# A two-layer trunk in split fp32: the second MLP matrices' first pairs taken as wide seven-product pairs

## The chip, the cores and the metric

One Trainium2 chip, one core. The metric is the device time of one execution in microseconds (us); the kernel is launched once and computes the whole reference. TensorE is called PE (PEld is its weight load), VectorE DVE, ScalarE ACT, GpSimd POOL, and SyncE SP; nearly all loads are issued from SP.

## The reference

256 rows of 2048 channels go through two layers, all in float32. Cut to its steps:

```python
# layer 1
u = rms_norm(h, a_norm_g);  q, k, v, fz = split(u @ a_w_in)          # 2048 -> 3*2048+16
h = h + forgetting_attention(norm(q), norm(k), v, log_sigmoid(fz + b_f)) @ a_w_out
h = h + square(relu(rms_norm(h, g0) @ w1[0])) @ w2[0]                # 2048 -> 8192 -> 2048
# shared keys and values
k_sh, v_sh = split(rms_norm(h, kv_norm_g) @ kv_w)
# layer 2
q = norm(rms_norm(h, b_norm_g) @ b_w_q)
h = h + chunked_relbias_attention(q, norm(k_sh), v_sh, b_rel) @ b_w_out
h = h + square(relu(rms_norm(h, g1) @ w1[1])) @ w2[1]
```

The change concerns the second products (w2) of the two MLPs.

## The kernel before

**Products.** Weights are the moving operand of PE, 128 x 512 at a time; activations, transposed, are the stationary one, as 16 tiles x[0] to x[15] of 128 channels by 256 rows. Both are split into a part hi that PE takes exactly and the rest lo, and each product is made of three passes: hi by hi, hi weights by lo activations, lo weights by hi activations (lines L462, L464, L466, in `passes`). The weights are split as they arrive: ACT writes hi (L218) and DVE writes lo (L219). A **unit** is a block of weights of 128 x 1024 (512 KB) and takes 12 matmuls: two channel tiles, two row halves, three passes. There are three buffers for hi and three for lo of whole units, and one each for half blocks (`hih`, `loh`). `top_up` splits up to three units ahead; raw units are loaded through four buffers.

**Pairs.** An MLP goes through four chunks c of 2048 hidden channels. Each chunk has four pairs: two of w1 (q = 0, 1), then two of w2 (q = 0, 1). A pair makes two neighbouring results of 512 columns, a and b, over 16 input tiles. On the first input tiles it uses seven products of block sums in place of eight (Winograd's form of Strassen's method) on four blocks of weights "11", "12", "21", "22". The blocks' sums are formed on chip: T3 = 22 + 12, T2 = T3 + 11, T1 = 12 + 11, T4 = 21 + T2. The seven products come as **forms** f0 to f6 in the order 11, T3, T2, T1, 21, T4, 22. The activations' sums for them are called S (w1) and Sh (w2).

- A **narrow** pair does this on four tiles (x[0] to x[3]): f0 to f6 of 6 matmuls each, then the ordinary units a2 to a7 and b2 to b7. Blocks have 512 KB, and all four sums are added by DVE (`make`, L811).
- A **wide** pair does it on six tiles (x[0] to x[5]): each form f_i is followed by a half form h_i of 3 matmuls on a half block; the ordinary units are a3 to a7 and b3 to b7. Blocks have 768 KB. DVE makes T3 and T2, of 128 x 1536; T1 and T4 are made by transfers on POOL's queue that add a block from memory onto the one on chip (`put`, L817).

`WIDE1` and `WIDE2` say which pairs of w1 and w2 are wide: before, all of w1 but the first, and in w2 those with q = 1. The w2 pairs with q = 0, one in each chunk, are narrow.

**Order.** `Pair.plan` writes out the order of units; b5, b6, b7 of a pair come between the first forms of the next pair. The start of a wide pair after a w1 pair reads: ... a7 b3 b4 of the old pair, f0 h0, b5 of the old, f1 h1, b6, f2 h2, b7, f3 h3, then a3 of the new pair. `when` gives for "12", "22", "21", "11", T3, T1 how many ordinary units ahead of the pair's f0 each is loaded or made (`prepare`). `keep_order` makes DVE, ACT, PE and SP keep the written order.

**Hidden activations.** A result of w1 gives a quarter n (0 to 3) of the chunk's hidden tiles: n = 0 and 1 from a and b of the first w1 pair, 2 and 3 from the second. Quarter n holds tiles x[4n] to x[4n+3]. When its sums are done, `turn_hidden` transposes it on DVE (L330), sends it through memory and back, and runs the steps of `take`: relu (ACT, L830), square into hi (ACT, L835), square in place (ACT, L837), lo (DVE, L841), and for n = 0 and 1 four differences (DVE, L285 to L288), their hi part (ACT, L292) and lo part (DVE, L295) in Sh. `uses` says after which ordinary unit each step is written; the numbers count from the transposes.

Of the kernel before, what the change touches and what calls it, by code (L numbers as in the profile page):

```python
# [31 lines left out]
REL = 384  # L32
WIDE = UN + 512
WIDE1 = (1, 2, 3, 4, 5, 6, 7)
WIDE2 = (1, 3, 5, 7)


def keep_order(tc, engines):
# [8 lines left out]


@with_exitstack
def trunk(ctx: ExitStack, tc: tile.TileContext, xT, xr, gs, hg, bf, wgate, w_in, w_oa, w1a, w1fa, w1sa, w2a, w2fa, w2sa,  # L50
          w_kv, w_qb, w_ob, w1b, w1fb, w1sb, w2b, w2fb, w2sb, rel, out):
    nc = tc.nc
    V, S, G, TE, SY = nc.vector, nc.scalar, nc.gpsimd, nc.tensor, nc.sync

# [47 lines left out]
    def queue(src, m):  # L102
        u = [src[i] for i in range(m)]
        n = KT // UA
        u[: 2 * n] = [u[i + q * n] for i in range(n) for q in range(2)]
        units.extend(u)
# [13 lines left out]
    class Pair:  # L120
# [9 lines left out]

        def plan(self, rest):
            made = [self.items(f"f{i} h{i}" if self.wide else f"f{i}") for i in range(7)]
            own = {"early": "a2 F a3 F b2 F b3 a4 b4 a5 a6 a7", "": "a2 F a3 F a4 F a5 a6 a7 b2 b3 b4",
                   "late": "a2 F a3 F b2 F b3 a4 a5 b4 a6 a7", "wide": "a3 F b3 F a4 F b4 a5 a6 a7", "ahead": "a3 F a4 F a5 F a6 a7 b3 b4"}[self.order].split()
            plan = made[0] + rest[:1] + made[1] + rest[1:2] + made[2] + rest[2:] + made[3]
            n = 4
            for i in own:
                if i == "F":
                    plan += made[n]
                    n += 1  # L140
                else:
                    plan += self.items(i)
            return plan, self.items("b5 b6 b7")

    def plan_mlp(w1, w1f, w1s, w2, w2f, w2s, tail):
        pairs = []

        def add(w, wf, ws, i, wides, order, when):
            j = wides.index(i) if i in wides else i - sum(1 for k in wides if k < i)
            names = ("11", "12", "21", "22")  # L150
            if i in wides:
                src = [[None] * 3 + [ws[10 * j + 5 * q + u] for u in range(5)] for q in range(2)]
                big = {k: wf[4 * j + m] for m, k in enumerate(names)}
            else:
                src = [[w[16 * j + 8 * q + u] for u in range(8)] for q in range(2)]
                big = {k: src[int(k[1]) - 1][int(k[0]) - 1] for k in names}
            pairs.append(Pair(big, src, order, len(pairs) % 2 == 0, when, i in wides))

        close = (7, 5, 6, 4, 3, 2)
        for c in range(NCH):  # L160
            for q in range(2):
                i = 2 * c + q
                order = "ahead" if i in WIDE1 else "" if i else "early"
                when = (25, 20, 9, 15, 10, 8) if not i else (9, 7, 8, 6, 3, 2) if i == 1 else close if i - 1 in WIDE1 or not q else (9, 7, 8, 6, 5, 1)
                add(w1, w1f, w1s, i, WIDE1, order, when)
            for q in range(2):
                i = 2 * c + q
                add(w2, w2f, w2s, i, WIDE2, "wide" if q else "late", close if q or i + 1 in WIDE1 else (9, 7, 8, 6, 5, 2))
        plan, rest = [], [(tail, 0, u) for u in range(KT // UA - 3, KT // UA)]
        for p in pairs:  # L170
            mine, rest = p.plan(rest)
            plan += mine
        plan += rest
        units.extend(Form(p, i, q == 3) if q > 1 else p.src[q][i] for p, q, i in plan)
        return plan

# [2 lines left out]
    n_out = w_oa.shape[0] - 3  # L179
    queue(w_oa, n_out)  # L180
    tail_a = Tail(w_oa, n_out - 5)
    plan_a = plan_mlp(w1a, w1fa, w1sa, w2a, w2fa, w2sa, tail_a)
    queue(w_qb, w_qb.shape[0])
    for i in range(w_kv.shape[0]):
        units.append(w_kv[i])
    queue(w_ob, n_out)
    tail_b = Tail(w_ob, n_out - 5)
    plan_b = plan_mlp(w1b, w1fb, w1sb, w2b, w2fb, w2sb, tail_b)
    ready = deque()

    raws = deque()
# [106 lines left out]
    def room(tag, name, dtype=F32):  # L298
        return qkv.tile([P, WIDE], dtype, name=name, tag=tag, bufs=1 if tag == "bias" else 2)
# [18 lines left out]
    def steps(make):  # L318
        box = []

        def step():
            if not box:
                box.append(make())
            next(box[0])
        return step

    def blocks32(src, z, b):
        n = src.shape[1] // P
        nb = z.shape[1] // (n * P)
        V.transpose(z.rearrange("p (j n b c) -> p b n j c", j=4, n=n, b=nb)[:, b],  # L330
                    src.rearrange("p (n j c) -> p n j c", n=n, j=4))

    def carry(z, dst, wait=1):
        w = z.shape[1]
        n = w // 4
        box = []

        def rows():
            box.append(dram.tile([P, w], F32, name="turn", tag=f"turn{w}", bufs=4))
            SY.dma_start(box[0], z)  # L340

        def columns():
            s = box[0].rearrange("(i a) f -> a i f", i=4)
            d = dst.rearrange("p (i f) -> p i f", i=4)
            for j in range(4):
                SY.dma_start(d[32 * j : 32 * j + 32], s[:, :, j * n : (j + 1) * n])

        return [[rows]] + [[]] * wait + [[columns], [], []]

    def turned(name=None):  # L350
        z = qkv.tile([P, GH * T], F32, name="z")
        return (z, qkv.tile([P, GH * T], F32, name=name, tag=name, bufs=2)) if name else z
# [52 lines left out]
    class RowStats:  # L405
# [4 lines left out]
        def add(self, b, n):  # L410
            t = wk.tile([P, 512], F32, name="sqr", tag="wk")
            S.activation(t, h[b][:, n * 512 : (n + 1) * 512], AF.Square, accum_out=self.ss[:, b * NG + n : b * NG + n + 1])
# [250 lines left out]
    def add_fill(items):  # L663
        for i, it in enumerate(items):
            if i < len(fill):
                fill[i] = fill[i] + it
            else:
                fill.append(it)
# [35 lines left out]
    early = room("bias", "early")  # L704
# [75 lines left out]
    for g in range(NG):  # L780
        zq, lq = turned("z")
        qb = {}
        late = 6 if g == 0 else 0
# [35 lines left out]
    def prepare(p, d):  # L819
        for name, at in zip(("12", "22", "21", "11", "T3", "T1"), p.units):  # L820
            if d == at:
                (bring if name[0] != "T" else put if p.adds and name == "T1" else make)(p, name)

    def mlp(plan, x, Sx, st, last):
        base = turns[0]
        hids = [[] for _ in range(NCH)]
        Sh = [[] for _ in range(NCH)]

        def take(t, c, n):
            S.activation(t, t, AF.Relu)  # L830
            y = acts.tile([P, 2, GH, T], F32R, name="act")
            hi, lo = (y[:, i].rearrange("p k (b i c) -> p (k b) i c", b=NB, i=4) for i in range(2))
            t3 = t.rearrange("p (i kb c) -> p kb i c", i=4, c=32)
            yield
            S.activation(hi, t3, AF.Square)  # L835
            yield
            S.activation(t, t, AF.Square)  # L837
            yield

            def low():  # L840
                V.tensor_tensor(lo, t3, hi.bitcast(F32), op=ALU.subtract)  # L841

            hids[c].extend(y[:, :, j, :] for j in range(GH))
            low()
            yield
            if n == 0:
                r = prob.tile([P, 9 * 3 * P], F32R, name="Sh", tag="p", bufs=1)
                Sh[c].extend(r[:, i : i + n] for i, n in ((0, UN), (UN, UN), (2 * UN, 512), (2 * UN + 512, 512)))
                yield from sums([[t3[:, 2 * j + b :: 4] for j in range(2)] for b in range(NB)], Sh[c])
            elif n == 1:  # L850
                yield from sums([[t3[:, 2 * j + b : 2 * j + b + 1] for j in range(2)] for b in range(NB)], Sh[c][2:], 1)

        def turn_hidden(c, n):
            zt = []

            def f(b, ps):
                if b == 0:
                    zt.extend(turned("q"))
                blocks32(ps, zt[0], b)
                if b == NB - 1:  # L860
                    step = steps(lambda: take(zt[1], c, n))
                    uses = ((4, 5, 7, 8, 9, 10, 11), (4, 5, 6, 7, 8, 10, 15), (4, 5, 7, 8), (4, 5, 6, 6))[n]
                    if not c and n < 2:
                        uses = (5, 6, 7, 8, 8, 10, 15) if n else (4, 5, 6, 7, 8, 9, 10)
                    add_fill(carry(*zt, 0)[:2] + [[step] * uses.count(i) for i in range(3, uses[-1] + 1)])
            return f

# [192 lines left out]
```

## Time and profile before

| what | value |
|---|---|
| median of 3 runs (lowest, highest) | 2097.52 us (2096.82, 2102.56) |
| the profiled execution's own time | 2096.35 us |
| its span on the core | 2094.6 us |
| PE busy | 2087.4 us, 9266 records |
| DVE, ACT busy | 1606.3 us, 1233.0 us |
| mean transfer rate | 251 GB/s |

The profile tells one execution. A timeline row holds the start in us from the span's start, the duration of the group, engine, line, operation, out<-in, how many, and in brackets the idle time before it and what ended it. Consecutive rows of PE overlap, because matmuls are pipelined: the step from one start to the next is what a matmul costs, and the 389 ns of a group row is its latency. On DVE the step from one start to the next is also a little shorter than the duration.

### The profile page before, as it was taken

To read this page: it belongs to the slowest core of one execution; us is meant where nothing else is said; L and a number is where in the kernel's file an instruction comes from. 1 tells how busy PE (TensorE), PEld (TensorE's weight loads), DVE (VectorE), ACT (ScalarE), POOL (GpSimd) and SP (SyncE) were. 2 spreads that over 40 slices of the span, in tenths; PEclk is the share of its full clock that TensorE was granted. 3 is DMA by queue.
4 is the path that set the end of the run, shared out by engine and by line. 5 is a ranking of instruction groups with operands and counts; after the bars stand their busy time and mean duration, and the time that the engine had idled before them with its cause. 6 is when DMAs were issued, how large, how long until landed. Compare 5 with 4: busy or idle time off the path is not lost.

```text
span 2094.6 us, 26203 instructions
## 1 busy us (share of the span) xinstructions
PE 2087.4 (100%) x9266; PEld 1726.7 (82%) x9266; DVE 1606.3 (77%) x1920; ACT 1233.0 (59%) x1583; POOL 98.2 (5%) x107
## 2 busy tenths in 40 slices
PE   9999999999999999999999999999999999999999
PEld 7888888888888888888888888887888888888887
DVE  6767666888788778878777677678977887788786
ACT  6544454776566566556675455456755665665664
POOL 1111000000000000000001010000000000000000
PEclk9999999999999999999999999999999999999999
DMA  7787778778787897787778777788787887878875
GB/s 287 246 257 242 228 255 266 250 253 276 250 265 236 260 277 251 220 276 271 230 233 263 236 233 232 240 268 256 250 279 250 243 261 256 269 244 247 275 265 152
DMA packets 181205, 526.25 MB, mean 251 GB/s; under 512 B 36801, under 2 KB 72017, under 8 KB 181073
## 3 DMA queue, kind: packets, MB, share of 16 engines
q1 hardware_dynamic: 173552, 484.69, 68.3%
q0 software_dynamic: 7520, 39.87, 10.2%
q8 instruction: 73, 1.20, 0.2%
q14 instruction: 60, 0.48, 0.1%
HBM read 484.62 MB, written 39.87 MB: 250 GB/s over the span
## 4 chain that ended last, share of the span: by engine, by line
PE 98%; DMA 1%; ACT 0%; DVE 0%; SPq 0%; issue 0%; DVEq 0%; ACTq 0%
PE acc L462 26%; PE acc L464 26%; PE acc L466 26%; PE s L466 6%; PE s L462 6%; PE s L464 6%; PE s L605 1%; PE po L635 1%; DMA raw<-in_w1b 0%; PE s L604 0%; PE po L636 0%; DMA raw<-in_w_in 0%; PE s L727 0%; ACT hi L218 0%; DVE lo L219 0%; DVE act L310 0%
## 5 line engine op out<-in xcount | busy, mean ns | idle before, releaser
L219 DVE TENSOR_TENSOR lo<-raw,hi 128x1024 fp32r<-128x1024 f32 (+1 forms) x598 | 724.7, 1216 | 241.5 <-ACT hi L218 227.0
L218 ACT ACTIVATE hi<-raw 128x1024 fp32r<-128x1024 f32 (+1 forms) x598 | 628.6, 1052 | 318.1 <-PE acc L464 231.7
L462 PE MATMUL acc<-hi,act 128*128 128x512 f32 x2154 | 593.1, 394 | 2.0 <-ACT act L309 1.1
L464 PE MATMUL acc<-hi,act 128*128 128x512 f32 x2154 | 583.8, 389 | 0.1
L466 PE MATMUL acc<-lo,act 128*128 128x512 f32 x2154 | 583.2, 389 | 0.1
L464 PEld LDWEIGHTS acc<-hi,act 128*128 128x128 f32 x2154 | 403.9, 188 | 85.7 <-DVE act L310 0.7
L466 PEld LDWEIGHTS acc<-lo,act 128*128 128x128 f32 x2154 | 403.8, 188 | 85.2 <-DVE lo L219 1.4
L462 PEld LDWEIGHTS acc<-hi,act 128*128 128x128 f32 x2154 | 401.7, 188 | 85.6 <-ACT hi L218 1.7
L218 ACT ACTIVATE hi<-w 128x1024 fp32r<-128x1024 f32 x138 | 145.6, 1055 | 126.3 <-DMA w<-in_w1fb 26.8
L219 DVE TENSOR_TENSOR lo<-w,hi 128x1024 fp32r<-128x1024 f32 x138 | 167.6, 1214 | 54.5 <-ACT hi L218 48.6
L219 DVE TENSOR_TENSOR lo<-wT,hi 128x1024 fp32r<-128x1024 f32 x86 | 104.9, 1219 | 37.0 <-ACT hi L218 36.6
L462 PE MATMUL s<-hi,act 128*128 128x512 f32 x424 | 114.7, 389 | 0.0
L466 PE MATMUL s<-lo,act 128*128 128x512 f32 x424 | 114.6, 389 | 0.0
L464 PE MATMUL s<-hi,act 128*128 128x512 f32 x424 | 114.6, 389 | 0.0
L218 ACT ACTIVATE hi<-wT 128x1024 fp32r<-128x1024 f32 x86 | 90.8, 1056 | 24.8 <-PE acc L464 13.0
L464 PEld LDWEIGHTS s<-hi,act 128*128 128x128 f32 x424 | 79.6, 188 | 16.5
L466 PEld LDWEIGHTS s<-lo,act 128*128 128x128 f32 x424 | 79.4, 188 | 16.7 <-DVE lo L219 0.2
L462 PEld LDWEIGHTS s<-hi,act 128*128 128x128 f32 x424 | 79.5, 188 | 16.5
L218 ACT ACTIVATE hih<-w 128x512 fp32r<-128x512 f32 x88 | 55.2, 627 | 61.0 <-PE acc L464 50.0
L219 DVE TENSOR_TENSOR loh<-w,hih 128x512 fp32r<-128x512 f32 x88 | 60.4, 687 | 19.8 <-ACT hih L218 19.8
L218 ACT ACTIVATE hih<-wT 128x512 fp32r<-128x512 f32 x66 | 41.4, 628 | 57.2 <-PE acc L464 47.9
L638 ACT ACTIVATE act<-po 128x256 fp32r<-128x256 f32 x32 | 12.3, 385 | 86.2 <-PE po L636 86.2
(207 smaller groups left out, 1835.4 us busy)
## 6 DMA issues: line engine op xcount, KB each, us to landing
raw<-in_w_in SPq DMA_DIRECT2D x96, 512.0 KB, 4.5
raw<-in_w1sa SPq DMA_DIRECT2D x70, 512.0 KB, 5.5
raw<-in_w1sb SPq DMA_DIRECT2D x70, 512.0 KB, 5.8
raw<-in_w_kv SPq DMA_DIRECT2D x64, 512.0 KB, 4.6
turn<-z SPq DMA_DIRECT2D x60, 512.0 KB, 4.2
raw<-in_w2a SPq DMA_DIRECT2D x48, 512.0 KB, 5.2
raw<-in_w2b SPq DMA_DIRECT2D x48, 512.0 KB, 5.3
q<-turn SPq DMA_DIRECT2D x168, 128.0 KB, 3.8
```

What stands on the lines that cost most here:

```text
L218: S.activation(hi[:, c], raw[:, c], AF.Copy)
L219: V.tensor_tensor(lo[:, c], raw[:, c], hi[:, c].bitcast(F32), op=ALU.subtract)
L462: TE.matmul(ps[:, cols], xh, cut(hi, j), start=first, stop=False, **kw)
L464: TE.matmul(ps[:, cols], xl, cut(hi, j), start=False, stop=False, **kw)
L466: TE.matmul(ps[:, cols], xh, cut(lo, j), start=False, stop=last, **kw)
L605: TE.matmul(s[:, P : 3 * P], q[:, a, P:T], k[:, a], start=True, stop=True)
L635: TE.matmul(po[:, :T], v[:, 0, a * P : (a + 1) * P], pT[:, :2], start=True, stop=False)
L638: S.activation(o[i][:, 0], po[:, :T], AF.Copy)
```

## The change

All pairs of w2 become wide. Their half forms read tiles x[4] and x[5], that is quarter 1, and the Sh sums of quarter 1, from the pair's very start; `uses` therefore puts the steps of quarter 1 closer together, those of quarters 2 and 3 too, and in the first chunk those of quarter 0. Second, `when` loads block "21", the fifth form's, one ordinary unit ahead of a pair's f0 and no longer six (eight in the second pair of an MLP). The arrays for narrow w2 pairs and the orders "" and "late" go.

```diff
-WIDE2 = (1, 3, 5, 7)
+WIDE2 = (0, 1, 2, 3, 4, 5, 6, 7)
...
-            own = {"early": "a2 F a3 F b2 F b3 a4 b4 a5 a6 a7", "": "a2 F a3 F a4 F a5 a6 a7 b2 b3 b4",
-                   "late": "a2 F a3 F b2 F b3 a4 a5 b4 a6 a7", "wide": "a3 F b3 F a4 F b4 a5 a6 a7", "ahead": "a3 F a4 F a5 F a6 a7 b3 b4"}[self.order].split()
+            own = {"early": "a2 F a3 F b2 F b3 a4 b4 a5 a6 a7", "wide": "a3 F b3 F a4 F b4 a5 a6 a7", "ahead": "a3 F a4 F a5 F a6 a7 b3 b4"}[self.order].split()
...
-        close = (7, 5, 6, 4, 3, 2)
+        close = (7, 5, 1, 4, 3, 2)
         for c in range(NCH):
             for q in range(2):
                 i = 2 * c + q
-                order = "ahead" if i in WIDE1 else "" if i else "early"
-                when = (25, 20, 9, 15, 10, 8) if not i else (9, 7, 8, 6, 3, 2) if i == 1 else close if i - 1 in WIDE1 or not q else (9, 7, 8, 6, 5, 1)
+                order = "ahead" if i else "early"
+                when = (25, 20, 9, 15, 10, 8) if not i else (9, 7, 1, 5, 3, 2) if i == 1 else close
                 add(w1, w1f, w1s, i, WIDE1, order, when)
             for q in range(2):
                 i = 2 * c + q
-                add(w2, w2f, w2s, i, WIDE2, "wide" if q else "late", close if q or i + 1 in WIDE1 else (9, 7, 8, 6, 5, 2))
+                add(None, w2f, w2s, i, WIDE2, "wide", close)
...
-                    uses = ((4, 5, 7, 8, 9, 10, 11), (4, 5, 6, 7, 8, 10, 15), (4, 5, 7, 8), (4, 5, 6, 6))[n]
+                    uses = ((4, 5, 7, 8, 9, 10, 11), (4, 5, 6, 7, 7, 8, 8), (4, 5, 6, 7), (4, 5, 5, 5))[n]
                     if not c and n < 2:
-                        uses = (5, 6, 7, 8, 8, 10, 15) if n else (4, 5, 6, 7, 8, 9, 10)
+                        uses = (4, 5, 6, 7, 7, 8, 8) if n else (4, 4, 5, 6, 7, 8, 9)
```

In the changed file the lines after `plan` stand one or more lines higher, so L219 there is L218 and L841 is L840.

More of the change, by code (lines that the diff above doesn't have):

```diff
@@ L49, in trunk @@
 @with_exitstack
-def trunk(ctx: ExitStack, tc: tile.TileContext, xT, xr, gs, hg, bf, wgate, w_in, w_oa, w1a, w1fa, w1sa, w2a, w2fa, w2sa,
-          w_kv, w_qb, w_ob, w1b, w1fb, w1sb, w2b, w2fb, w2sb, rel, out):
+def trunk(ctx: ExitStack, tc: tile.TileContext, xT, xr, gs, hg, bf, wgate, w_in, w_oa, w1a, w1fa, w1sa, w2fa, w2sa,
+          w_kv, w_qb, w_ob, w1b, w1fb, w1sb, w2fb, w2sb, rel, out):
     nc = tc.nc
@@ L143, in plan, with plan_mlp @@
             return plan, self.items("b5 b6 b7")
-    def plan_mlp(w1, w1f, w1s, w2, w2f, w2s, tail):
+    def plan_mlp(w1, w1f, w1s, w2f, w2s, tail):
         pairs = []
@@ L181, in trunk @@
     tail_a = Tail(w_oa, n_out - 5)
-    plan_a = plan_mlp(w1a, w1fa, w1sa, w2a, w2fa, w2sa, tail_a)
+    plan_a = plan_mlp(w1a, w1fa, w1sa, w2fa, w2sa, tail_a)
     queue(w_qb, w_qb.shape[0])
@@ L187, in trunk @@
     tail_b = Tail(w_ob, n_out - 5)
-    plan_b = plan_mlp(w1b, w1fb, w1sb, w2b, w2fb, w2sb, tail_b)
+    plan_b = plan_mlp(w1b, w1fb, w1sb, w2fb, w2sb, tail_b)
     ready = deque()
@@ L1033 @@
         "w1sa": m1[0][2],
-        "w2a": m2[0][0],
         "w2fa": m2[0][1],
@@ L1042 @@
         "w1sb": m1[1][2],
-        "w2b": m2[1][0],
         "w2fb": m2[1][1],
```

## The prediction

> **What bounds the kernel now.** I read the page first (span, share of each engine, the chain that ended last), then the waits of PE alone, then the timeline of PE at the starts of three pairs.
>
> ```profile
> span 2094.6 us, 26203 instructions
> ...
> PE 2087.4 (100%) x9266; PEld 1726.7 (82%) x9266; DVE 1606.3 (77%) x1920; ACT 1233.0 (59%) x1583; POOL 98.2 (5%) x107
> ...
> PEclk9999999999999999999999999999999999999999
> ...
> PE 98%; DMA 1%; ACT 0%; DVE 0%; SPq 0%; issue 0%; DVEq 0%; ACTq 0%
> ```
> ```profile
> PE acc L462 <- ACT act L309: 1.1, 1, 1.1
> PE pt L91 <- DVE mhalf L93: 1.1, 1, 1.1
> PE acc L462 <- ACT hi L218: 0.8, 1, 0.8
> ```
> ```profile
> 618.66 1.07 PE L462 MATMUL acc<-hi,act 128*128 128x512 f32 x4
> ...
> 621.38 1.07 PE L462 MATMUL acc<-hi,act 128*128 128x512 f32 x4
> ...
> 624.10 0.62 PE L462 MATMUL s<-hi,act 128*128 128x512 f32 x2
> ...
> 666.28 0.62 PE L462 MATMUL acc<-hi,act 128*128 128x512 f32 x2
> ...
> 707.76 0.62 PE L462 MATMUL s<-hi,act 128*128 128x512 f32 x2
> ```
>
> PE carries 98% of the chain, and its named waits come to 3 us. So a matmul less shortens the span, and a wait of PE lengthens it one for one. An ordinary unit of 12 matmuls takes 621.38 - 618.66 = 2.72 us: one matmul occupies PE for 0.227 us, a whole form (6 matmuls) for 1.36 us, a half form (3) for 0.68 us. At 624.10 stands f0 of the second chunk's first second-matrix pair (narrow now), at 666.28 f0 of the next pair (wide already), at 707.76 that of the one after. Narrow takes 42.18 us, wide 41.48 us.
>
> **Part 1, fewer matmuls.** A narrow pair has 7 x 6 + 12 x 12 = 186 matmuls, a wide one 7 x 9 + 10 x 12 = 183. Eight pairs change (four chunks in each of two MLPs): 24 matmuls, and by the two stretches above 8 x (42.18 - 41.48) = 5.6 us, **-5.6 us**. Beside that, the narrow starts have a few short waits in front of the passes over Sh, which this row of the view of tile Sh gives (who ended its engine's idle time, us, times):
>
> ```profile
>   DVE lo L219: 1.4, 5
> ```
> They go with the narrow starts: **-1.4 us**.
>
> **Part 2, the start of those eight pairs.** Here DVE decides. DVE works in written order, and its work for a start begins when PE ends the previous pair's a7, because the transposes (L330) wait for that result. PE from there runs b3, b4, f0, h0, b5, f1, h1. One start is wide today and has these transposes too, that of the second chunk's second first-matrix pair: f0 at 582.62, so b3 at 577.18. The timelines of DVE and PE there:
>
> ```profile
> 576.93 1.31 DVE L330 STREAM_TRANSPOSE z<-acc 128x512 f32<-128x512 f32 x2 [0.85 <-PE acc L466]
> 578.17 1.72 DVE L811 TENSOR_TENSOR wT<-w,w 128x1536 f32<-128x1536 f32 x1
> 579.80 1.22 DVE L219 TENSOR_TENSOR lo<-w,hi 128x1024 fp32r<-128x1024 f32 x1
> 580.94 0.69 DVE L219 TENSOR_TENSOR loh<-w,hih 128x512 fp32r<-128x512 f32 x1
> 581.54 1.22 DVE L219 TENSOR_TENSOR lo<-raw,hi 128x1024 fp32r<-128x1024 f32 x1
> 583.06 1.23 DVE L219 TENSOR_TENSOR lo<-wT,hi 128x1024 fp32r<-128x1024 f32 x1 [0.30 <-ACT hi L218]
> 585.30 0.69 DVE L219 TENSOR_TENSOR loh<-wT,hih 128x512 fp32r<-128x512 f32 x1 [1.01 <-ACT hih L218]
> 586.03 1.76 DVE L811 TENSOR_TENSOR wT<-wT,w 128x1536 f32<-128x1536 f32 x1
> 587.71 1.22 DVE L219 TENSOR_TENSOR lo<-raw,hi 128x1024 fp32r<-128x1024 f32 x1
> ```
> ```profile
> 582.62 0.62 PE L462 MATMUL acc<-hi,act 128*128 128x512 f32 x2
> ...
> 584.21 0.39 PE L464 MATMUL acc<-hih,act 128*128 128x512 f32 x1
> ...
> 588.97 0.39 PE L464 MATMUL acc<-hih,S 128*128 128x512 f32 x1
> ```
>
> In order on DVE: transposes, T3, the lo of f0, of h0, of b5, of f1, of h1, then T2, then the lo of b6. The changed program (its written order) puts this sequence at the eight starts, and inside it the work for the hidden activations, whose prices stand at today's narrow start and in one group row:
>
> ```profile
> 622.36 1.29 DVE L295 TENSOR_TENSOR Sh<-sum,Sh 128x512 fp32r<-128x512 f32 x2
> 623.56 1.22 DVE L811 TENSOR_TENSOR w<-w,w 128x1024 f32<-128x1024 f32 x1
> ...
> 625.83 1.22 DVE L841 TENSOR_TENSOR act<-q,act 128x1024 fp32r<-128x1024 f32 x1
> 626.97 1.22 DVE L219 TENSOR_TENSOR lo<-wT,hi 128x1024 fp32r<-128x1024 f32 x1
> ...
> 630.50 0.29 DVE L285 TENSOR_TENSOR sum<-q 128x128 f32<-128x128 f32 x1
> ...
> 631.43 1.22 DVE L219 TENSOR_TENSOR lo<-wT,hi 128x1024 fp32r<-128x1024 f32 x1
> ```
> ```profile
> L295 DVE TENSOR_TENSOR Sh<-sum,Sh 128x512 fp32r<-128x512 f32 x24 | 15.8, 684 | 0.0
> ```
>
> From start to start: the two Sh lo parts of quarter 0 take 1.20 us, L841 1.14 (1.22 to its end), the four differences 0.93. The new order is: transposes, T3, lo of f0, **two Sh lo parts**, lo of h0, lo of b5, **L841 of quarter 1**, **four differences**, lo of f1, lo of h1, T2, lo of b6, **Sh lo part of quarter 1**. Laid on the wide start above:
>
> L841 begins at 581.54 + 1.13 (a lo of 1024 from start to start) + 1.20 = 583.87 and ends at 585.09. It makes the lo of tile x[4], which a narrow pair first multiplies in a2, after the forms, and a wide pair in h0. The second matmul of h0, at 584.21, reads it: PE stands 0.88 us.
>
> The differences follow from 585.01, the lo of f1 from 585.94, of h1 from 587.08, T2 from 587.81 (lo of h1 and the step to T2: 0.73), the lo of b6 from 589.49 (T2: 1.68), the last Sh lo part from 590.62 to 591.30. The second matmul of h1, at 588.97, reads it: PE stands **2.33 us** in all at this start, 0.88 of them in h0 and 1.45 in h1. Behind both waits stands all that PE has queued, and ACT's half of h1's block waits for h0, with about 1 us to spare in the new order (h1's lo is not due on DVE before 587.08). No later work of PE gives the time back, since PE itself is the bound.
>
> Whether block "11", the operand of f0, still lands in time when it has 768 KB is not shown; ACT's timeline at the narrow start and two rows of the DMA view bound it:
>
> ```profile
> 620.12 1.06 ACT L218 ACTIVATE hi<-w 128x1024 fp32r<-128x1024 f32 x1 [1.83 <-DMA w<-in_w2a]
> ```
> ```profile
> w<-in_w2fa SPq DMA_DIRECT2D x16, 768.0 KB, 7.8
> ...
> w<-in_w2a SPq DMA_DIRECT2D x16, 512.0 KB, 6.4
> ```
> Today it lands 620.12 - 618.66 = 1.46 us after b3 begins, and the new order wants f0's hi from 579.80 - 577.18 - 1.06 - 0.04 = 1.52 us on. By the medians the larger block takes 1.4 us more, but block "21" (512 KB), now ahead of it in the queue, leaves. So it is 0 to 1.34 us late, which goes into DVE's chain one for one. I take 0.3, nearer the low end, since the queue in front of it gets no longer. A start then costs 2.2 us (the chain, with 0.1 for hand-overs that may overlap) to 3.7 us (the chain and the latest landing), taken as 2.63: eight cost **+21.0 us**.
>
> A rule that speaks against such stalls is about the clock. The longest that PE stood inside the MLPs is this, on its timeline:
>
> ```profile
> 1449.88 1.20 PE L462 MATMUL acc<-hi,act 128*128 128x512 f32 x4 [1.08 <-ACT act L309]
> ```
> It left the granted clock at 9 tenths or more in its slice, as in every other. Stalls of 0.88 and 1.45 us are of that size, so I charge nothing for the clock. The Trainium skill, "TensorE: Matmul & The Clock Gate", section "Why this matters for your kernels", says to leave no idle gap of PE over about 3 us, because one idle window returns the clock to half. By that rule too these stalls stay free, unless the two of one start count as one; that case is rival D.
>
> **Part 3, the rest, at nothing.** Quarter 3's L841 now comes in a5, and a6 reads it. Its squares have this row:
>
> ```profile
> L835 ACT ACTIVATE act<-q 128x1024 fp32r<-128x1024 f32 x32 | 33.5, 1046 | 0.0
> ```
> From b4's start: a buffer is free at 1.81 (8 of 12 matmuls), a split and two squares of this size take 3 x 1.05 less overlap, 3.05, L841 1.22, so it is ready at 6.1; a6 wants it at 2 x 2.72 + 0.91 = 6.35. The cover is 0.2 us; without it, up to 0.3 x 8 = 2.4 us. The two POOL additions of a pair (T1, T4) are issued after T3 and after h2's lo; f3 and f5 come over 12 us later, and the same two additions hold up no PE work in today's wide pairs. Block "21", loaded one unit ahead, behind four column loads on SP, is split for f4, five forms and four units later: over 17 us against a landing of 7.8. DVE gets 56 more half lo parts and loses 48 instructions of 1024; away from the starts this falls into its idle 23%.
>
> **Sum.** 2096.35 (the profiled execution's time; its span is 2094.6) - 5.6 - 1.4 + 21.0 = 2110.4. The median of the runs shown lies 1.2 us above that execution, so **2111.5 us**, 0.67% slower.
>
> **Rivals.** (A) *The gain alone*: DVE reaches L841's end before h0 asks. The point is 7.03 us from b3's start (584.21 - 577.18); DVE needs 585.09 - 577.18 = 7.91. For it: today's wide starts run without such a wait. Against it: none of them has the Sh parts and L841 in front of h0. Then 2097.5 - 7.0 = 2090.5. (B) *Only h0 stands*: its 0.88 us, and DVE done sooner with h1's work than laid out, cover the last Sh part: 8 x 0.9 - 7.0, 2097.7, no change. (C) *Block "11" rules*: with the added transfers in the queue it is later than the medians say, 3.7 to 5 us a start: 2120 to 2131. (D) *The clock falls*: b5, f1, h1, b6 (33 matmuls, 7.5 us) run at half speed at each start: 2111 + 60 = 2171. That the change does not do what it says is no case: the built program has 24 matmuls less.
>
> **How the numbers follow.** Main case 0.78, A 0.06, B 0.06, C 0.08, D 0.02. The range runs from 2105 (a start of 1.8 us, for DVE work that overlaps more than laid out) to 2120 (3.7 us). 0.3%, 6.3 us, is about what a measurement of this kernel can tell from no change; A lies just past it, so a third of A is counted with B. Faster 0.04, same 0.08, slower 0.88.
>
> **What would show it.** Right: at each of the eight starts PE's half matmuls of h0 wait for DVE's L841 (one line less in the new file) about 0.9 us and those of h1 for L295 about 1.4 us, with 43 to 45 us from such an f0 to the next. Wrong: no wait there and 41.5 us (A); the first wait alone (B); ACT's split for f0 held by a landing for well over 2 us (C); a lower digit of PEclk (D); or a wait of PE in a6 for the last L841, where I charged nothing.

## The result, and the profile after

| kernel | median of its runs (lowest to highest) | ratio to before, 95% interval |
|---|---|---|
| before | 2097.94 us (2096.82 to 2102.56, 4 runs) | |
| changed | 2113.43 us (2111.38 to 2118.57, 4 runs) | 1.0072 [1.0058, 1.0085] |

The change makes the kernel 15.5 us slower; 2111.5 us, in a range of 2105 to 2120, was forecast. The profiled execution of the changed kernel is the slowest of its four, so its lines show some 5 us more than its median. Its page:

```profile
span 2116.8 us, 26314 instructions
...
PE 2091.2 (99%) x9242; PEld 1727.1 (82%) x9242; DVE 1615.5 (76%) x1944; ACT 1247.8 (59%) x1623; POOL 109.9 (5%) x123
...
PEclk9999999999999999999999999999999999999999
...
PE 94%; DMA 3%; DVE 2%; issue 0%; SPq 0%; ACT 0%; DVEq 0%; ACTq 0%
```

PE is busy 2091.2 us against 2087.4 before, with 24 records fewer, and its share of the chain that ended last fell from 98% to 94%: DVE and transfers now stand in that chain. What they hold up is in the view of PE's waits (engine, tile and line that waits, what it waits for; us in total, times, longest):

```profile
PE s L463 <- DVE act L840: 14.3, 8, 2.7
PE s L463 <- DVE Sh L294: 5.7, 5, 1.1
...
```

These two lines were not there before. They are the two waits that the prediction named, in h0 for the lo of quarter 1 (L840) and in h1 for its last Sh lo part (L294), one each at the eight starts; at three starts the second is missing. The timelines of PE and DVE at the first of the eight:

```profile
458.43 0.62 PE L461 MATMUL s<-hi,act 128*128 128x512 f32 x2
...
459.79 0.39 PE L461 MATMUL s<-hih,act 128*128 128x512 f32 x1
460.96 0.50 PE L463 MATMUL s<-hih,act 128*128 128x512 f32 x1 [0.78 <-DVE act L840]
...
465.63 0.39 PE L461 MATMUL s<-hih,Sh 128*128 128x512 f32 x1
467.16 0.50 PE L463 MATMUL s<-hih,Sh 128*128 128x512 f32 x1 [1.14 <-DVE Sh L294]
```
```profile
452.74 1.31 DVE L329 STREAM_TRANSPOSE z<-acc 128x512 f32<-128x512 f32 x2 [0.85 <-PE acc L465]
453.98 1.72 DVE L810 TENSOR_TENSOR wT<-w,w 128x1536 f32<-128x1536 f32 x1
455.62 1.21 DVE L218 TENSOR_TENSOR lo<-w,hi 128x1024 fp32r<-128x1024 f32 x1
456.75 1.28 DVE L294 TENSOR_TENSOR Sh<-sum,Sh 128x512 fp32r<-128x512 f32 x2
457.95 0.68 DVE L218 TENSOR_TENSOR loh<-w,hih 128x512 fp32r<-128x512 f32 x1
458.56 1.22 DVE L218 TENSOR_TENSOR lo<-raw,hi 128x1024 fp32r<-128x1024 f32 x1
459.69 1.21 DVE L840 TENSOR_TENSOR act<-q,act 128x1024 fp32r<-128x1024 f32 x1
460.83 0.28 DVE L284 TENSOR_TENSOR sum<-q 128x128 f32<-128x128 f32 x1
...
461.75 1.22 DVE L218 TENSOR_TENSOR lo<-wT,hi 128x1024 fp32r<-128x1024 f32 x1
462.89 0.68 DVE L218 TENSOR_TENSOR loh<-wT,hih 128x512 fp32r<-128x512 f32 x1
463.61 1.76 DVE L810 TENSOR_TENSOR wT<-wT,w 128x1536 f32<-128x1536 f32 x1
465.28 1.22 DVE L218 TENSOR_TENSOR lo<-raw,hi 128x1024 fp32r<-128x1024 f32 x1
466.42 0.69 DVE L294 TENSOR_TENSOR Sh<-sum,Sh 128x512 fp32r<-128x512 f32 x1
```

From one matmul's start to the next's PE takes 0.227 us where nothing holds it. What is beyond that is lost: 460.96 - 459.79 - 0.23 = 0.94 us in h0 and 467.16 - 465.63 - 0.23 = 1.30 in h1. After each stall the next matmul again comes 0.11 late. So this start loses **2.46 us**. DVE has no gap from its transposes to L294: it is its queue that PE waits for. By this count, start-to-start time beyond 0.227 us, used below for all kernels, the eight starts of this execution lose 28.1 us and all other places in the MLPs 2.1; before it was 3.8 in all. 24 matmuls less are 5.45 us, so the span should grow by 30.2 - 3.8 - 5.45 = 21.0 us; it grew by 2116.8 - 2094.6 = 22.2.

The starts are not alike: the first and the last lose 2.46, the six between 3.45 and 4.35. The second of them, on ACT, DVE and PE:

```profile
624.39 1.06 ACT L217 ACTIVATE hi<-w 128x1024 fp32r<-128x1024 f32 x1 [3.09 <-DMA w<-in_w2fa]
```
```profile
621.43 1.31 DVE L329 STREAM_TRANSPOSE z<-acc 128x512 f32<-128x512 f32 x2 [0.85 <-PE acc L465]
622.67 1.72 DVE L810 TENSOR_TENSOR wT<-w,w 128x1536 f32<-128x1536 f32 x1
625.49 1.23 DVE L218 TENSOR_TENSOR lo<-w,hi 128x1024 fp32r<-128x1024 f32 x1 [1.10 <-ACT hi L217]
```
```profile
630.85 0.50 PE L463 MATMUL s<-hih,act 128*128 128x512 f32 x1 [1.97 <-DVE act L840]
631.19 0.40 PE L465 MATMUL s<-loh,act 128*128 128x512 f32 x1
631.43 1.64 PE L461 MATMUL acc<-hi,act 128*128 128x512 f32 x4
```

Block "11" landed at 624.4, ACT had stood 3.09 us for it, and DVE stood 1.10 us between T3 and the lo of f0, in the middle of the chain; at all six such starts DVE stood so, 0.90 to 1.81 us. h0 loses 2.13 us. Then four matmuls take 1.64 us where they take 1.07: PE runs at half clock, which the page's digits, a mean over 53 us each, don't show. Stretches of the view by windows do (window, its length, PE busy, PEld, DVE, ACT, POOL, then the granted clock, the DMA share and GB/s):

```profile
628.30:631.70 3.40, 1.43 (x7) 0.86 (x6) 3.37 (x8) 0.83 (x2) 0.00 (x0) 1.00 1.03 229
631.80:635.10 3.30, 3.30 (x10) 2.53 (x9) 3.27 (x3) 1.69 (x3) 0.00 (x0) 0.50 1.09 283
```
```profile
1679.70:1683.00 3.30, 1.53 (x8) 0.94 (x7) 3.27 (x7) 0.74 (x2) 0.00 (x0) 1.00 0.99 203
1683.10:1686.40 3.30, 3.30 (x17) 2.70 (x16) 3.27 (x4) 1.92 (x3) 0.00 (x0) 1.00 1.11 245
```

Behind the second start the clock is 0.50 for one window; behind the sixth, at 1683, with a stall of 1.93 us, it stays 1.00. Three of the eight starts have such a stretch, and they are the three without a wait in h1, since DVE catches up while PE runs slowly.

### The profile page after: what moved, and what is told of

Same layout as the page of the kernel before. It is cut to its first block, busy times and chain, and to the rows that moved or that the text cites. A ratio compares the mean times of both kernels' runs of the same rounds, so it can differ in the third digit from the quotient of the medians.

```text
span 2116.8 us, 26314 instructions
## 1 busy us (share of the span) xinstructions
PE 2091.2 (99%) x9242; PEld 1727.1 (82%) x9242; DVE 1615.5 (76%) x1944; ACT 1247.8 (59%) x1623; POOL 109.9 (5%) x123
## 4 chain that ended last, share of the span: by engine, by line
PE 94%; DMA 3%; DVE 2%; issue 0%; SPq 0%; ACT 0%; DVEq 0%; ACTq 0%
PE acc L463 25%; PE acc L461 25%; PE acc L465 24%; PE s L463 6%; PE s L465 6%; PE s L461 6%; DVE lo L218 1%; DMA w<-in_w2fa 1%; PE s L604 1%; PE po L634 1%; DMA q<-turn 1%; DMA raw<-in_w2sb 0%; DMA w<-in_w2fb 0%; PE s L603 0%; PE po L635 0%
## 5 line engine op out<-in xcount | busy, mean ns | idle before, releaser
L218 DVE TENSOR_TENSOR lo<-raw,hi 128x1024 fp32r<-128x1024 f32 (+1 forms) x582 | 705.0, 1215 | 235.5 <-ACT hi L217 222.1
L217 ACT ACTIVATE hi<-raw 128x1024 fp32r<-128x1024 f32 (+1 forms) x582 | 611.5, 1052 | 288.3 <-PE acc L463 214.7
L461 PE MATMUL acc<-hi,act 128*128 128x512 f32 x2122 | 586.5, 395 | 0.7 <-ACT hi L217 0.5
L463 PE MATMUL acc<-hi,act 128*128 128x512 f32 x2122 | 578.2, 391 | 0.0
L218 DVE TENSOR_TENSOR lo<-w,hi 128x1024 fp32r<-128x1024 f32 x130 | 157.8, 1214 | 33.7 <-ACT hi L217 33.5
L218 DVE TENSOR_TENSOR lo<-wT,hi 128x1024 fp32r<-128x1024 f32 x94 | 114.6, 1219 | 75.4 <-ACT hi L217 74.2
L217 ACT ACTIVATE hih<-w 128x512 fp32r<-128x512 f32 x120 | 75.2, 627 | 74.3 <-PE acc L463 63.3
L217 ACT ACTIVATE hih<-wT 128x512 fp32r<-128x512 f32 x90 | 56.5, 628 | 95.7 <-PE acc L463 63.3
L461 PE MATMUL s<-hi,act 128*128 128x512 f32 x392 | 106.2, 389 | 0.0
L463 PE MATMUL s<-hi,act 128*128 128x512 f32 x392 | 106.1, 389 | 0.0
L218 DVE TENSOR_TENSOR loh<-w,hih 128x512 fp32r<-128x512 f32 x120 | 82.3, 686 | 22.0 <-ACT hih L217 22.0
L463 PEld LDWEIGHTS s<-hi,act 128*128 128x128 f32 x392 | 73.6, 188 | 15.3
L461 PEld LDWEIGHTS s<-hi,act 128*128 128x128 f32 x392 | 73.5, 188 | 15.2
L218 DVE TENSOR_TENSOR loh<-wT,hih 128x512 fp32r<-128x512 f32 x90 | 61.9, 688 | 19.4 <-ACT hih L217 19.4
```

The costliest lines, as they stand in the source:

```text
L217: S.activation(hi[:, c], raw[:, c], AF.Copy)
L218: V.tensor_tensor(lo[:, c], raw[:, c], hi[:, c].bitcast(F32), op=ALU.subtract)
L461: TE.matmul(ps[:, cols], xh, cut(hi, j), start=first, stop=False, **kw)
L463: TE.matmul(ps[:, cols], xl, cut(hi, j), start=False, stop=False, **kw)
```

## The experiments

Four questions: are both waits DVE's queue, and only that? What does the late block cost? What does the later load of "21" do by itself? And does the gain of 5.6 us exist, if the starts lose nothing? Before ran beside every one, at 2098.7 us (the first four), 2098.4 (the next three), 2098.3 (the next two) and 2099.5 (the last). Of each edit only the parts of lines that differ are printed.

**Block "21" back where it was**, in the changed kernel.

```diff
-close = (7, 5, 1, 4, 3, 2)
+close = (7, 5, 6, 4, 3, 2)
-(9, 7, 1, 5, 3, 2) if i == 1
+(9, 7, 8, 5, 3, 2) if i == 1
```


> The changed kernel with block 21 loaded six units ahead again (eight in the second pair), everything else kept. If DVE's chain and the landing of block 11 in front of it make the stalls: 21, now 768 KB, goes ahead of 11 in the queue, 11 lands 1 to 1.9 us later at each of the eight starts, and the time is 2121 to 2128 us. If the landing plays no part and only DVE's order counts: as the changed kernel, 2111 to 2116. If loading 21 late was itself what cost: towards 2091 to 2100.

Measured: 2133.57 us, ratio 1.0166 [1.0145, 1.0186], more than any theory said. ACT's split of f0 at the second start and PE's waits:

```profile
628.03 1.06 ACT L217 ACTIVATE hi<-w 128x1024 fp32r<-128x1024 f32 x1 [3.49 <-DMA w<-in_w2fa]
```
```profile
PE s L463 <- DVE act L840: 20.3, 8, 3.1
PE s L463 <- DVE Sh L294: 3.4, 3, 1.1
PE acc L463 <- DVE act L840: 2.7, 3, 1.2
PE acc L461 <- ACT act L308: 2.7, 2, 2.3
```

"11" lands 2.3 us before f0 begins (at 630.35), where it was 2.7 in the changed kernel (627.13 - 624.39): 0.4 us later at this start, where the theory had 1 to 1.9. The eight starts lose 35.7 us for 28.1, five half-clock stretches behind them included, and other places of the MLPs 10.2 for 2.1: a6 (third line), passes that wait for ACT, and a sixth half-clock stretch behind one of these. So in the wide kernel the late load of "21" is worth 20 us by the medians; of the 15.7 us that the two profiles show of it, half lies away from "11" and the starts.

**Only "21" late**, in the kernel before.

```diff
-close = (7, 5, 6, 4, 3, 2)
+close = (7, 5, 1, 4, 3, 2)
-(9, 7, 8, 6, 3, 2) if i == 1
+(9, 7, 1, 5, 3, 2) if i == 1
```


> The kernel before with only the other part of the change: block 21 loaded one unit ahead. DVE-chain theory: no wait of PE hangs on it, 2095 to 2099 us, no change (the short waits at w2 starts may go, up to 1 us). If the move of 21 on SP's queue were a cause of the stalls: over 2103.

Measured: 2094.46 us, ratio 0.9978 [0.9969, 0.9988]. The time lost in the MLPs falls from 3.8 to 1.75 us. This half of the change is a small gain, just below the 2095 to 2099 us expected of no change, and 0.2% the other way from the sum.

**Quarter 1's steps one unit earlier**, in the changed kernel.

```diff
-(4, 5, 6, 7, 7, 8, 8)
+(3, 4, 5, 6, 6, 7, 7)
```


> The changed kernel with the seven steps of quarter 1 written one ordinary unit earlier each. Block 11 as it is. DVE-chain theory: L840 then ends at 6.2 us after b3's start where h0 asks at 7.0, the last Sh lo part stands before the lo of f1, so the wait in h1 goes and in h0 about 0.5 us (for its loh) and the lateness of block 11 (0 to 1.9 us) stay: 2098 to 2104 us. If the stalls came from block 11's landing alone: 2110 to 2114, as the landing is unchanged. If ACT's relu, now one unit earlier, waits for the transposed columns, DVE waits too and part of the gain is missing: 2104 to 2110.

Measured: 2114.35 us, ratio 1.0074 [1.0051, 1.0097]: nothing gained. PE's waits, and ACT at the second start:

```profile
PE s L465 <- DVE loh L218: 8.3, 8, 1.0
PE s L463 <- DVE act L840: 6.7, 7, 1.4
```
```profile
616.20 1.06 ACT L829 ACTIVATE q<-q 128x1024 f32<-128x1024 f32 x1 [2.09 <-DMA q<-turn]
```

The wait for L294 is gone, as forecast. But the relu now comes before quarter 1 is back from memory: ACT stands 2.09 us, with the splits of a7 and b3 behind it, and DVE behind those. And the lo of h0 now stands behind L840 and the differences, so h0 waits for it as well. The forecast overlooked both. By its time alone this run would also fit the rival, stalls from the landing of "11"; the two waits for DVE in h0 speak against that, and the next run tells the two apart.

**Block "11" ahead of "22"**, in the changed kernel.

```diff
-close = (7, 5, 1, 4, 3, 2)
+close = (7, 5, 1, 6, 3, 2)
-(9, 7, 1, 5, 3, 2) if i == 1
+(9, 5, 1, 6, 3, 2) if i == 1
```


> The changed kernel with block 11 loaded six units ahead, before block 22 (five), where it was four. Quarter 1 as in the change. DVE-chain theory: only the lateness goes, and all eight starts stall like the two in the profile where DVE did not wait for 11, 2.46 us each: 2097.9 - 7 + 19.7 = 2108 to 2111 us, with L840 and L294 as releasers at all eight and no clock drop. If the landing were the cause: 2091 to 2096.

Measured: 2112.83 us (2110.38 to 2112.96), ratio 1.0069 [1.0045, 1.0093]. The profiled run is the one of 2110.38.

```profile
PE s L463 <- DVE Sh L294: 9.1, 8, 1.1
PE s L463 <- DVE act L840: 6.3, 8, 0.8
```

That is 2 us above what was expected of the median; the profiled run is where it was expected. In it the starts are alike, each loses 2.45 to 2.48 us, eight 19.7, and no stretch has half the clock. This is DVE's chain without a late block. Against the changed kernel's median it gains 0.6 us only, less than the spread of either. The lateness that cost 8 us in the profile shown above need not be as large in other executions: the other three of the changed kernel are 4 to 7 us shorter than the profiled one. The next kernels start from this order of the loads.

**Quarter 0's last steps two units earlier**, so that its two Sh lo parts leave the chain.

```diff
-((4, 5, 7, 8, 9, 10, 11), (4, 5, 6, 7, 7, 8, 8)
+((4, 5, 6, 7, 8, 8, 9), (4, 5, 6, 7, 7, 8, 8)
-if n else (4, 4, 5, 6, 7, 8, 9)
+if n else (4, 4, 5, 6, 7, 7, 8)
```


> The changed kernel with block 11 in front of block 22, as in the experiment before, and with the last steps of quarter 0 two units earlier (its lo one, its differences, their hi and lo parts two), so that its two Sh lo parts (1.20 us of VectorE) stand before the transposes and no longer between the lo of f0 and the lo of h0. Theory (VectorE's chain behind the transposes sets the loss of 2.46 us at each of the eight starts): h0 waits no more, since its 0.8 to 0.9 us are less than 1.20, h1 waits 1.26 us for the last Sh lo part; 2112.8 - 8 x 1.20 = 2103 us (2101 to 2105). Rival (VectorE is full in front of the transposes too, so what is moved there only puts the transposes off): between 612 and 621 us of the last run it idles 0.26 + 0.83 + 0.20 us, so at worst nothing is gained, 2112 to 2113 us, with the transposes beginning over 1 us after TensorE's last pass of a7. Rival (another wait takes its place, ScalarE's square of quarter 1 or a buffer): 2108 us or more, and another line behind TensorE's waits in h0.

Measured: 2109.80 us, ratio 1.0056 [1.0037, 1.0075]: 3 of the 9.6 us. Six starts lose 0.33 + 0.11 us in h0 and some 1.4 in h1. The other two, the first of each MLP, lose 3.9 and 4.1, with T3 late (at the first ACT's split of f1 waits 1.11 us for it). DVE's timeline at the second start:

```profile
617.95 2.36 DVE L218 TENSOR_TENSOR lo<-raw,hi 128x1024 fp32r<-128x1024 f32 x2 [1.65 <-ACT hi L217]
620.23 1.29 DVE L294 TENSOR_TENSOR Sh<-sum,Sh 128x512 fp32r<-128x512 f32 x2
621.44 1.22 DVE L218 TENSOR_TENSOR lo<-raw,hi 128x1024 fp32r<-128x1024 f32 x1
622.57 1.31 DVE L329 STREAM_TRANSPOSE z<-acc 128x512 f32<-128x512 f32 x2
```

The transposes have no idle time in front any more (0.85 us in the changed kernel): they wait for DVE, not for PE. The earlier Sh hi parts stand on ACT ahead of two splits, and cost DVE 1.65 us of idling. That is the rival in the main, with a third of the gain won: work was moved to where DVE had little room.

**T3 one unit earlier**, for the first w2 pairs.

```diff
-add(None, w2f, w2s, i, WIDE2, "wide", close)
+add(None, w2f, w2s, i, WIDE2, "wide", close if q else (7, 6, 1, 5, 4, 2))
```


> The changed kernel with block 11 in front of block 22 for the pairs of w1 and the second w2 pairs, and for the eight first w2 pairs T3 made one unit earlier (four units ahead of f0, no longer three) from block 22 loaded six and block 11 five units ahead. T3 (1.63 us from start to start) then stands before the transposes. Theory (VectorE's chain): h0's wait of 0.8 to 0.9 us goes, h1's 1.6 shrinks by the rest, 2.46 - 1.63 = 0.83 us a start; 2112.8 - 13 = 2099.8 us (2098 to 2102). Rival (full in front too): VectorE idles 0.83 + 0.20 us in the last 2.7 us ahead of the transposes, so a gain of 1.0 us a start, 2104.6 us. Rival (block 22 or 11 lands late where T3 or the split of f0 wants it, which stops all VectorE work behind it): 2110 us or more, with VectorE's T3 ended by a transfer.

Measured: 2102.14 us (10 runs), ratio 1.0013 [1.0003, 1.0024]. PE's waits, and DVE at the second start:

```profile
PE s L463 <- DVE Sh L294: 8.2, 8, 1.1
```
```profile
616.65 1.75 DVE L810 TENSOR_TENSOR wT<-w,w 128x1536 f32<-128x1536 f32 x1
618.32 1.22 DVE L218 TENSOR_TENSOR lo<-raw,hi 128x1024 fp32r<-128x1024 f32 x1
619.45 1.31 DVE L329 STREAM_TRANSPOSE z<-acc 128x512 f32<-128x512 f32 x2
```

h0's wait is gone at all eight, h1 loses 1.28: a gain of 10.7 us, between the theory's 13 and the rival's 8. T3 moved by 1.67 us and filled the 0.85 us that DVE idled there; the rest put the transposes off by about 0.5 (5.2 us ahead of f0, 5.7 in the changed kernel).

**Both edits together.**

> The last two edits in one kernel: quarter 0's last steps two units earlier and T3 one unit earlier for the first w2 pairs. 2.83 us of VectorE leave the chain, more than the 2.46 us lost at a start. Theory (VectorE's chain is all that the starts lose): no wait at any of the eight starts, about 41.5 us from such an f0 to the next; 2112.8 - 8 x 2.46 = 2093 us (2089 to 2095), faster than the kernel before by some 0.25% or more. Rival (full in front too): of the 2.83 us only what VectorE idles from 604 to 620 us of the earlier run can be won, and with the order of ScalarE's work only the last 1.3 us of it: 2100 to 2104 us. Rival (a further cost that all wide pairs have, beside the starts): 2097 us or more with no wait at the starts.

Measured: 2105.84 us, ratio 1.0034 [1.0021, 1.0048]: worse than T3 alone. Six starts lose 1.85 us and two 2.27, in h0 and h1, for the reason that the kernel with quarter 0 showed: DVE idles 1.65 us for ACT again, and the transposes begin only 3.4 us ahead of f0. Only work that fits a gap is moved for nothing.

**The last Sh part of quarter 1 right behind its differences**, with "11" first, without and with the earlier T3.

```diff
-(4, 5, 6, 7, 7, 8, 8)
+(4, 5, 6, 7, 7, 7, 7)
```


> The changed kernel with block 11 in front of block 22, and with the last two steps of quarter 1 (the hi part and the lo part of its differences) one unit earlier, right behind the differences: the last Sh lo part then stands on VectorE before the lo of f1 and h1, T2 and the lo of b6, no longer behind them. T3 stays where the change has it. Theory (the two waits of a start are two places in VectorE's order): h0's 0.95 + 0.11 us stay, h1's 1.30 + 0.11 go; 2112.8 - 8 x 1.41 = 2101.5 us (2100 to 2104). Rival (the loss is VectorE's total work at a start, whatever its order, and ScalarE's answer to the differences now makes VectorE idle 0.6 to 0.9 us more): TensorE stands later, in the last pass of f1, h1 or b6, for as long: 2112 to 2119 us.

Measured: 2102.85 us (10 runs), ratio 1.0019 [1.0009, 1.0030]. In the profile L294 has left PE's waits, and six starts lose 0.94 + 0.11 us in h0 and 0.28 in b6, 1.34 instead of 2.46. The other two, at 459 and 1502 us, lose 3.28 and 1.82; at the first, a raw block landed late and ACT stood 3.12 us for it.

> The same edit together with T3 one unit earlier for the first w2 pairs (blocks 22 and 11 six and five units ahead), the kernel that ran at 2102.1 us with 1.28 us lost a start, all of it in h1. Theory: that wait goes, and no new one comes, since the lo of f1 is due on VectorE about 0.5 us before TensorE's last pass of f1 asks for it; 2102.1 - 8 x 1.28 = 2092 us (2089 to 2095), faster than the kernel before, and its first pairs run from start to start in 41.5 us. Rival (a new wait in f1, h1 or b6, since VectorE idles for ScalarE and T2 and the lo of b6 come 1.5 us later): 2097 us or more, with the lo of b6 or of f1 behind TensorE's waits. Rival (wide pairs cost something that no wait shows): 2097 us or more without waits at the starts.

Measured: 2093.25 us (12 runs), ratio **0.9977 [0.9966, 0.9987]**, faster than before. Seven starts lose 0.11 us, one 1.15.

```profile
PE acc L463 <- DVE act L840: 1.7, 3, 1.0
...
PE s L463 <- DVE act L840: 0.6, 1, 0.6
```

The two edits each take out one wait, and together both: h0 and h1 are two places in one queue. The first line is a6.

**Quarter 3's square one unit earlier**, in that kernel.

```diff
-(4, 5, 6, 7), (4, 5, 5, 5))
+(4, 5, 6, 7), (4, 4, 5, 5))
```


> The kernel that ran at 2093.25 us, with quarter 3's first square (ScalarE) one unit earlier, right behind its relu, where ScalarE idled 0.94 us before the split of a7's block. In that kernel, as in the changed one, TensorE loses 0.19 us or more in a6 of each first w2 pair, waiting for quarter 3's lo (1.32 us where a raw block landed late); eight such losses came to 3.7 us in its profile. Theory (the loss in a6 is ScalarE's work between relu and lo): the lo is ready about 1 us earlier, the 0.19 us losses go, the large ones shrink by some 0.8 us; 2093.25 - 2.5 = 2090.8 us (2089.5 to 2092.5). Rival (a landing sets it, or the square only puts off the split of a7 and with it VectorE's lo and T3): 2093 us or more, with the losses in a6 as before or new ones at the starts.

Measured: **2089.78 us** (2089.68 to 2091.29, 5 runs), ratio **0.9959 [0.9946, 0.9973]**, 9.8 us faster than before. The losses in a6 are gone but for one of 0.35 us. In part the rival shows too: at the starts three lose 0.38 to 1.34 us (at the largest, ACT had stood 1.89 us for a raw block) and five 0.11. The page, and one pair from f0 to the next f0:

```profile
span 2089.5 us, 26319 instructions
...
PE 2081.9 (100%) x9242; PEld 1722.9 (82%) x9242; DVE 1615.8 (77%) x1944; ACT 1249.5 (60%) x1623; POOL 111.6 (5%) x123
```
```profile
623.75 0.61 PE L461 MATMUL s<-hi,act 128*128 128x512 f32 x2
...
665.40 0.62 PE L461 MATMUL acc<-hi,act 128*128 128x512 f32 x2
```

41.65 us, against 42.18 for the narrow pair and 44.26 for the changed kernel's first one. The span is 5.1 us below that of before, about what 24 matmuls are worth. The rest of the 9.8 lies between the profiled executions and the medians: the profiled one of before took 3.2 us less than the median of the runs beside this kernel, that of this kernel 1.5 us more than its own. The late "21" has a share in the gain: against the kernel with only that, which ran at 0.9978 of before, the ratio is 0.9981, some 4 us (a comparison across two sets of runs), and between the two profiles the span falls by 3.4 us, 2092.9 to 2089.5. That is the 5.45 us of the matmuls less some 2 us that the starts of the last kernel lose more. So the gain of Part 1 exists, and this kernel keeps most of it.

## Why the prediction was right

- **Fewer matmuls, -5.6.** Right: 24 x 0.227 = 5.45 us, and the last kernel's pair of 41.65 us has 0.53 of the 0.68 that three matmuls are worth; one hand-over of 0.11 is the most of what is missing.
- **Short waits at the narrow starts, -1.4.** Half of it, by start-to-start time: the passes over Sh at the narrow starts lost 0.7 us before. The row that gave 1.4 sums idle time of the weight loads (PEld) ahead of those passes; half of that is hidden beside running matmuls, and PE's own waits have no such row.
- **Eight starts, +21.0.** The step that carried the forecast. The order laid out on DVE is the order in the trace, and the waits are where it put them: h0 0.94 us for a forecast of 0.88, h1 1.30 for 1.45, two restarts of 0.11 that were not in it, 2.46 for 2.33. Moving T3 alone took the first wait away, moving the Sh part alone took the second (and left 0.28 in b6), and moving both took both, so this is shown and not only argued.
- **Block "11", 0.3 a start of it.** The bound was 0 to 1.34. In the profiled run DVE stood 0.90 to 1.81 us for it at six starts, over the bound at two, and these six lost 1.0 to 1.9 us more than the two that had none. Between the two orders of loading it comes to 0.6 us in all by the medians and 2.0 by the means of four runs each, 0.1 to 0.25 a start. So the term is not far off for a typical run, as far as four runs can tell, and the upper bound was too low for single starts. What it took for granted, that taking "21" away helps the larger blocks, fits the 20 us that "21" costs in its old place.
- **The clock, nothing.** Right in size, wrong in its reason. The digits of the page that it went by are 9 throughout in the changed kernel too, and yet half-clock stretches occur there, behind stalls of h0 alone of 2.1 to 2.8 us, which need a late block on top of the chain. They cost little, since at half rate for 3.41 us PE loses 1.6 us while DVE catches up the 1.4 of h1: those three starts lose 0 to 0.2 us more than their h0 wait and an h1 wait would together. Rival D, with 60 us, held neither in extent nor in price.
- **a6, nothing with 0.2 us of cover.** Missed by 0.19 us a pair, 1.5 us in eight (within the 2.4 that it was bounded with). It shows as start-to-start time, 0.08 + 0.11, with no wait in brackets; in the later kernels single losses reach 1.3, where a raw block lands late on ACT in front of the squares.
- **"21" one unit ahead, nothing.** It was priced for itself only, as in time for f4, which it is. What it frees was used for the bound on "11", but not where it helps the kernel before: 2 us in the profile, 0.2% in the medians.
- **Rivals.** The gain alone (A, 2090.5) is what the last kernel reaches, once DVE's work is moved and with the late "21" in the gain; in the change as it is DVE is 0.9 us late for h0, as the point of A said it would be. B fell, since h1 waits too. C, 3.7 to 5 us a start, describes four starts of the profiled run (3.85 to 4.35), and its sign, ACT's split for f0 held by a landing for well over 2 us, stands at five (2.88 to 3.79); the median it does not describe.
- **What was luck.** That the median came out within 2 us of the forecast is in part luck. Short waits (0.7 us too many), a6 (1.5 us too few) and "21" (about 2 us of gain left out) partly cancel, and block "11" cost anything from 0.6 us in all (medians) to 8 (the profiled run) for the 2.4 in the sum.

## What to carry to other kernels

When PE is the bound, a saving in its work is paid for where its operands are made: write the queue of the engine that makes them in order, from the event that releases it to the matmul that asks, and compare the two times. A share of 76% says nothing about such a place; here DVE had no gap for 14 us. To win the time back, move the one operation that has a gap waiting for it; the same edit that gained 10.7 us alone lost 3.7 of them when more was moved in front of it.

## What the runs showed of the hardware

The granted clock falls by a fixed grid. All 15 half-clock stretches in the 12 profiles, first and last microseconds of a run aside, last 3413 ns, and within one run their starts lie a whole number of 3413.3 ns apart (631.74, 1512.38 and 1853.71 in the changed kernel: 258 and 100 steps). Cut by that grid, every window from 30 us on in which PE idled 2.07 us or more was followed by a half-clock window, and none in which it idled 2.04 or less. Idle is here start-to-start time beyond 0.227 us; the busy times of the view by windows do not part the two so (1.66 us of PE in the window from 800.22 us of the kernel with quarter 1 earlier, before a half-clock one; 1.59 in that from 973.53 us of the kernel with "21" back, before a full one). The bound was read off these windows afterwards, and no run was made to test it. So the sixth start above, 1.93 us of stall and 2.04 idle in its window, stayed at full clock, and a stall of 2.46 us at 968 us did too, since a boundary of the grid cuts it: 1.2 us idle in one window, 1.4 in the next. The Trainium skill, "TensorE: Matmul & The Clock Gate", section "What's actually happening", has a window of 3413 ns that runs freely; the trace agrees to the digit. The rule that the prediction cited from the same page, no idle gap over about 3 us, is too lenient here: 2.07 us in one window were enough, in one piece or several.
